# A hybrid SSD and Conformer layer on one core: the second half's loads of split input weights, issued by ScalarE in place of SyncE

## The chip, the cores and the metric

The kernel runs on one core of a Trainium2 chip. The core has five engines, each with its own instruction stream that it works through in order: TensorE (PE: matmuls, with its weight loads as PEld), VectorE (DVE), ScalarE (ACT), GpSimd (POOL) and SyncE (SP), which here does nothing but issue transfers. Transfers (DMAs) run on 16 DMA engines beside them. An engine that issues a transfer first waits, in its own order, until the buffer that the transfer writes is free; the data lands later, and whoever reads it waits for a semaphore. A transfer issued by SP goes into one hardware queue (q1 on the profile's page), one issued by ACT into another (q10).

The metric is device time in microseconds (us) of one execution, and of several runs the median. A profile is of one execution of its own, which has its own time.

## What is computed

One layer over two sequences: 256 context tokens and 2048 latent tokens of width 1024 (18 tiles of 128 tokens). Cut to what matters:

```python
def trunk_layer(x, mod, ...):
    shift, scale, gate = jnp.split(mod, 3, axis=-1)
    h = rms_norm(x, g_pre) * (1 + scale) + shift
    u = h @ w_in
    z, xbc, dt_raw, ga, gb, gsil = jnp.split(u, [...], axis=-1)
    y_ssd, h_fin = ssd_branch(z, xbc, dt_raw, ...)     # conv of 5, scan in both directions, norm
    y_conf = conformer_branch(ga, gb, ...)             # ga * sigmoid(gb), conv of 31, layer norm, silu
    y_conf = y_conf * jax.nn.silu(gsil)
    out = jnp.concatenate([y_ssd, y_conf], axis=-1) @ w_out
    return x + gate * rms_norm(out, g_post), h_fin
```

The product `h @ w_in` is the part that the change touches: the weights that it reads.

## The kernel before

**Split operands.** The input product runs in a fast format, with each operand split into a high part and a low part: h into hh and hl, a weight tile into wh and wl. Each of eight steps over the width of 1024 takes three matmuls (lines 395 to 397): wh by hh, wh by hl, wl by hh.

**Weight tiles.** `w_in` is cut into 44 tiles of 128 columns (`WCOL`): 12 of xbc, 8 of ga, 8 of gb, 8 of z, 8 of gsil. A tile in its two parts takes 512 KB each.

**Two halves.** The tokens are worked in two halves (1280 and 1152 of them), since hh and hl of all do not fit. In the first half, `load_w` reads a tile from `in_w_in`, ScalarE rounds it to wh, VectorE subtracts for wl, and SyncE stores both to the buffers WHD and WLD in memory. In the second half, `load_w` only reads wh and wl back (lines 363 and 364): 44 pairs, 88 transfers.

**Buffers and lookahead.** wh and wl have three buffers each. `next_w` keeps the tile in use and the next two in them: when a unit of work starts, the pair of the tile two further on is asked for, into the buffers that the unit before has used. That load has to wait until PE's last matmul with the old tile is done.

**Units in the second half**, in the order of the program, each of two blocks of 512 tokens (b = 3 and 4), with 24 matmuls per tile and block:
- `xbc_unit` (xp): 12 tiles; ACT copies the sum to `raw` (line 480), then a convolution of 5 runs on ACT and DVE.
- `gab_unit`, 8 of them: tile gb and tile ga. For each block gb's matmuls, ACT's tanh (line 556, `gth`), ga's matmuls, DVE's product, and a store to GL (line 560). So the tiles of one unit are used in turn: gb, ga, gb, ga.
- `silu_unit` (sp), 16 of them: z and gsil, with ACT's tanh at line 571 (`sth`) and a store at line 573.

**What runs beside them.** Interleaved with the gab and z units are the scan over the half's nine latent tiles (`pass_a`) and the grid convolution. In `pass_a`, `load_lb` (line 680) has ACT issue a broadcast load of decay rows into `lb`; GpSimd masks it (692); ACT takes exponents of rows of it (689, tile `el`) and of all of it (700); DVE sums and multiplies (704, 705); PE multiplies with it (736, `py`); DVE closes the sum (777, tile `yg`). The scan's other loads, xT (667) and bc (669), its stores (766, 780) and all transfers of the convolution (kd at 632, cx at 633, the stores cv at 661) are issued by SP. ACT also copies the convolution's kernel rows, `kt` (641).

**What sets the order.** Outside the last stage a scheduler places instructions on each engine by a simulated time, so the order of an engine's stream is not the order of the code. An instruction moved to another engine can shift its new neighbours. Once built, each stream is fixed.

Of the kernel before, what the change touches and what calls it, by code (L numbers as in the profile page):

```python
# [84 lines left out]
def backbone_kernel(ctx, tc, xa, xt_in, cols, rows, wconv, conf_b, gp_row, bg_row, state0, w_mod, w_dt, w_in, w_out,  # L85
                    y_ctx, y_lat, new_state):
    nc = tc.nc
    G, DMA = nc.gpsimd, nc.sync
    V, S, T = (InOrder(tc, e) for e in (nc.vector, nc.scalar, nc.tensor))
# [8 lines left out]
    def dram(name, shape):  # L98
        return drp.tile(shape, F32, tag=name, name=name)
# [12 lines left out]
    WHD = [dram(f"whd{t}", [P, D]) for t in range(len(WCOL))]  # L112
    WLD = [dram(f"wld{t}", [P, D]) for t in range(len(WCOL))]
# [243 lines left out]
    def load_w(half, c0):  # L357
        t = WCOL.index(c0)
        wl = wp.tile([P, KT, P], F32R, tag="wl", name=f"wl{c0}_{half}", bufs=3)
        wh = wp.tile([P, KT, P], F32R, tag="wh", name=f"wh{c0}_{half}", bufs=3)  # L360
        flat = lambda w: w.bitcast(F32).rearrange("p k n -> p (k n)")
        if half:
            DMA.dma_start(flat(wh), WHD[t])
            DMA.dma_start(flat(wl), WLD[t])
            return wh, wl
        for u in range(2):
            ks = slice(4 * u, 4 * u + 4)
            wr = wp.tile([P, 4, P], F32, tag="wr", name=f"wr{c0}_{u}", bufs=2)
            DMA.dma_start(wr.rearrange("p k n -> p (k n)"), w_in[t * P:(t + 1) * P, u * 512:(u + 1) * 512])
            S.copy(wh[:, ks, :], wr)  # L370
            V.tensor_tensor(wl[:, ks, :], wr, wh[:, ks, :].bitcast(F32), SUB)
        DMA.dma_start(WHD[t], flat(wh))
        DMA.dma_start(WLD[t], flat(wl))
        return wh, wl
# [10 lines left out]
    def next_w():  # L385
        while len(wq) < 3 and wcols:
            wq.append(load_w(*wcols.pop(0)))
        return wq.pop(0)
# [726 lines left out]
    def conf_sum(i, n):  # L1115
        v = p2.tile([P, 8, P], F32, tag="v", name=f"v{i}", bufs=2)
        return v, sum8(v[:, 0, :], v[:, 0:4, :], n)
# [174 lines left out]
    v2, t = conf_sum(nx2, n2)  # L1292
# [23 lines left out]
    for a, i in enumerate(order[1:], 1):  # L1316
# [14 lines left out]
        if nx2 is not None:  # L1331
            st_load(nx2)
            v2, t = conf_sum(nx2, n2)
# [113 lines left out]
```

## Time and profile before

| what | value |
|---|---|
| runs of before | 1861.82, 1862.09 and 1856.99 us; median 1861.82 |
| profiled execution | 1866.34 us; span from the first to the last instruction 1864.3 us |
| PE busy over the span | 1809.9 us (97%) |
| DVE, ACT, POOL busy | 1211.3 (65%), 865.3 (46%), 168.4 us (9%) |
| mean granted PE clock | 0.986 |
| queue q1 (SP) | 335.56 MB, 57.8% of 16 engines' span |
| queue q10 (ACT) | 37.76 MB, 7.4% |
| second half's weight loads on SP | first issued at 738.6, last at 1376.5 us |

How to read it: a busy share is an average over stages with different limits, so what a change in one stage is worth is read from that stage. PE's busy time counts pipelined matmuls; the granted clock beside it says how fast they ran. A row of a wait names who waited, for whom, the total, the number of times and the longest. In a timeline a "q" behind an engine's name marks its sequencer, which issues a transfer; the time beside it is that of the issue and not that of the transfer.

### The profile page before, as it was taken

What the parts mean: (1) busy time and instruction counts of PE and PEld (TensorE: products, weight loads), DVE (VectorE), ACT (ScalarE), POOL (GpSimd) and SP (SyncE); (2) the same over time, 40 slices, a digit from 0 to 9 for tenths busy, and PEclk for the clock granted to TensorE, in tenths of its full rate; (3) what the DMA queues carried; (4) which work ended last, traced back from release to release, by engine and by line L of the source; (5) the groups of instructions that cost most, each with busy time, mean ns of one, the idle gap of its engine ahead of it and who ended that gap; (6) DMA issues with size and microseconds to landing.
All of it is one profiled execution on the core that took longest, in us unless ns stands there. A gap on an engine that the chain in (4) does not pass through costs nothing.

```text
span 1864.3 us, 29991 instructions
## 1 busy us (share of the span) xinstructions
PE 1809.9 (97%) x11223; PEld 1492.7 (80%) x11223; DVE 1211.3 (65%) x1841; ACT 865.3 (46%) x1956; POOL 168.4 (9%) x281
## 2 busy tenths in 40 slices
PE   7899999999999999999999989999999999999998
PEld 5788887888888888888887767777887888888886
DVE  2477867565767663587547475869347887777763
ACT  3646424443465441744235344554245545454441
POOL 0002001111111100100001011110000111111110
PEclk8999999999999999999999999999999999999999
DMA  8656565574686664546598879885877666566632
GB/s 299 220 202 207 206 230 187 171 241 151 212 282 227 222 210 160 164 156 201 171 225 234 184 219 230 236 234 196 276 233 247 180 185 171 171 171 171 186 102 79
DMA packets 305309, 375.21 MB, mean 201 GB/s; under 512 B 85255, under 2 KB 204679, under 8 KB 305165
## 3 DMA queue, kind: packets, MB, share of 16 engines
q1 hardware_dynamic: 284428, 335.56, 57.8%
q10 hardware_dynamic: 20736, 37.76, 7.4%
q8 instruction: 88, 1.44, 0.3%
q14 instruction: 57, 0.46, 0.1%
HBM read 243.66 MB, written 129.59 MB: 200 GB/s over the span
## 4 chain that ended last, share of the span: by engine, by line
PE 75%; DMA 12%; DVE 4%; issue 4%; ACT 3%; POOL 1%; SPq 1%; ACTq 0%; POOLq 0%; DVEq 0%
PE op L81 20%; PE sp L395 6%; DMA lb<-lt 6%; PE sp L396 6%; PE sp L397 6%; PE xp L395 4%; PE xp L396 4%; PE xp L397 4%; PE gb L395 2%; PE gb L397 2%; PE gb L396 2%; PE ga L395 2%; PE ga L396 2%; PE ga L397 2%; PE py L736 1%
## 5 line engine op out<-in xcount | busy, mean ns | idle before, releaser
L700 ACT ACTIVATE lb<-lb,WB 128x128 f32<-128x128 f32 x576 | 184.4, 391 | 169.7 <-POOL lb L692 162.5
L395 PE MATMUL sp<-hh,wh 128*128 128x512 f32 (+1 forms) x640 | 239.5, 374 | 0.0
L396 PE MATMUL sp<-hl,wh 128*128 128x512 f32 (+1 forms) x640 | 236.8, 370 | 0.0
L397 PE MATMUL sp<-hh,wl 128*128 128x512 f32 (+1 forms) x640 | 236.6, 370 | 0.0
L395 PE MATMUL xp<-hh,wh 128*128 128x512 f32 (+1 forms) x480 | 178.4, 373 | 6.0 <-ACT wh L370 3.1
L396 PE MATMUL xp<-hl,wh 128*128 128x512 f32 (+1 forms) x480 | 178.2, 372 | 0.0
L397 PE MATMUL xp<-hh,wl 128*128 128x512 f32 (+1 forms) x480 | 178.1, 371 | 0.0
L692 POOL TENSOR_SCALAR_AFFINE_SELECT lb<-lb 128x512 f32<-128x512 f32 x144 | 105.7, 737 | 736.2 <-ACT el L689 412.0
L492 DVE SCALAR_TENSOR_TENSOR cva<-raw,cwh,cva 128x1280 f32<-128x1280 f32 (+1 forms) x96 | 141.6, 1483 | 19.7 <-ACT cva L486 17.7
L395 PEld LDWEIGHTS sp<-hh,wh 128*128 128x128 f32 x640 | 121.4, 190 | 20.6
L397 PEld LDWEIGHTS sp<-hh,wl 128*128 128x128 f32 x640 | 121.2, 189 | 20.9
L396 PEld LDWEIGHTS sp<-hl,wh 128*128 128x128 f32 x640 | 121.3, 190 | 19.9
L395 PE MATMUL ga<-hh,wh 128*128 128x512 f32 (+1 forms) x320 | 121.3, 379 | 6.1 <-DMA wh<-whd 6.1
L75 DVE SCALAR_TENSOR_TENSOR cg<-cg,cv 128x256 f32<-128x256 f32 x240 | 121.2, 505 | 3.4
L395 PE MATMUL gb<-hh,wh 128*128 128x512 f32 (+1 forms) x320 | 121.0, 378 | 2.4 <-DVE gth L559 2.4
L397 PE MATMUL ga<-hh,wl 128*128 128x512 f32 (+1 forms) x320 | 119.6, 374 | 0.1
L397 PE MATMUL gb<-hh,wl 128*128 128x512 f32 (+1 forms) x320 | 119.6, 374 | 0.0
L396 PE MATMUL gb<-hl,wh 128*128 128x512 f32 (+1 forms) x320 | 119.5, 373 | 0.0
L396 PE MATMUL ga<-hl,wh 128*128 128x512 f32 (+1 forms) x320 | 119.2, 372 | 0.0
L704 DVE TENSOR_TENSOR lb<-lb,lb 128x512 f32<-128x512 f32 x72 | 51.2, 711 | 92.9 <-ACT lb L700 77.1
L395 PEld LDWEIGHTS xp<-hh,wh 128*128 128x128 f32 x480 | 91.5, 191 | 23.5 <-ACT wh L370 3.9
L396 PEld LDWEIGHTS xp<-hl,wh 128*128 128x128 f32 x480 | 91.0, 190 | 15.3 <-DVE hl L316 0.4
(254 smaller groups left out, 3744.7 us busy)
## 6 DMA issues: line engine op xcount, KB each, us to landing
lb<-lt ACTq DMA_DIRECT2D x144, 256.0 KB, 4.4
wr<-in_w_in SPq DMA_DIRECT2D x88, 256.0 KB, 5.2
whd<-wh SPq DMA_DIRECT2D x44, 512.0 KB, 3.3
wld<-wl SPq DMA_DIRECT2D x44, 512.0 KB, 5.1
wh<-whd SPq DMA_DIRECT2D x44, 512.0 KB, 5.4
wl<-wld SPq DMA_DIRECT2D x44, 512.0 KB, 5.9
xT<-xb SPq DMA_DIRECT2D x18, 512.0 KB, 4.1
yp<-yg SPq DMA_DIRECT2D x36, 256.0 KB, 6.0
```

What stands on the lines that cost most here:

```text
L75: return self._tc.keep_in_program_order(getattr(self._eng, name)(*a, **k))
L81: return lambda *a, **k: self._tc.keep_in_program_order(f(*a, **k))
L395: T.matmul(ps[:, :BN], wh[:, k, :], hh[:, k, :], start=(k == 0), stop=False)
L396: T.matmul(ps[:, :BN], wh[:, k, :], hl[:, k, :], start=False, stop=False)
L397: T.matmul(ps[:, :BN], wl[:, k, :], hh[:, k, :], start=False, stop=(k == KT - 1))
L492: V.scalar_tensor_tensor(a[:, :n], raw[:, t:t + n], cwh[:, ct * 5 + t:ct * 5 + t + 1], a[:, :n], MUL, ADD)
L692: G.affine_select(E[g, hq, d], E[g, hq, d], pattern=[[0, 4], [sg, P]], compare_op=ALU.is_ge, fill=NEG, base=0, channel_multiplier=-sg)
L700: S.activation(lb[:, h, :], lb[:, h, :], AF.Exp, bias=WB[:, i, c + h:c + h + 1])
L704: V.tensor_tensor(a, a, E[g, hq, 1], ADD)
L736: T.matmul(py[g][j * HD:(j + 1) * HD, q * P:(q + 1) * P], xt[g][:, h * HD:(h + 1) * HD], E[g, hq, 0][:, t, :], start=True, stop=True)
```

## The change

Two lines of `load_w`: in the second half the pair is issued by ACT (`S`) and no longer by SP (`DMA`).

```diff
         if half:
-            DMA.dma_start(flat(wh), WHD[t])
-            DMA.dma_start(flat(wl), WLD[t])
+            S.dma_start(flat(wh), WHD[t])
+            S.dma_start(flat(wl), WLD[t])
             return wh, wl
```

All sizes, buffers and the first half stay. PE's stream keeps its order but for three groups of small matmuls of the step sizes that stand two or four matmuls later. Names in the rows below end in numbers of the buffer or tile: whd_137 and wld_181 are the parts of the fifth further ga tile (GA5; GA0 is whd_132), whd_146 is GB6, whd_136 GA4, whd_145 GB5.

ACT's stream where the pair of GA5 stands now, ahead of the tanh of the fifth gab unit's second block (gth_4_4); rows with + are new there:

```order
 L700 ACTIVATE lb_10434<-lb_10434,WB 128x128 x4
 L680 DMA lb_10109<-lt_116 128x512
+L363 DMA wh_1_9664<-whd_137 128x1024
+L364 DMA wl_1_9663<-wld_181 128x1024
 L556 ACTIVATE gth_4_4_10015<-gb_4_4_9890 128x512
 L689 ACTIVATE el_9876<-lb_10109 64x256 x2
 L680 DMA lb_10179<-lt_116 128x512
```

The pair stands between an lb load and the tanh that waits for the same block of matmuls as the pair does; the next lb load is four rows behind it.

SP's stream at the same place in the program, from which the pair of GA5 and the one of GB6 are taken; a row with - is gone from where it stood:

```order
 L632 DMA kd_10813<-in_wconv 32x1024 x3
 L669 DMA bc_10330<-xb_64 128x4x128
-L363 DMA wh_1_9664<-whd_137 128x1024
-L364 DMA wl_1_9663<-wld_181 128x1024
+L766 DMA st_108<-sb_10074 128x512
 L780 DMA yp_90<-yg_9703 128x512
-L766 DMA st_108<-sb_10074 128x512
-L363 DMA wh_1_10125<-whd_146 128x1024
-L364 DMA wl_1_10124<-wld_190 128x1024
 L667 DMA xT_10328<-xb_64 128x8x128
 L560 DMA gl_72<-gth_4_4_10015 128x512
```

GA5's pair stood behind the convolution's kd loads and the scan's bc load; without the pairs the scan's two stores change places, and xT and gl follow at once.

ACT's stream one unit earlier, where the pair of GA4 stands now, in the new order alone:

```order
L700 ACTIVATE lb_10111<-lb_10111,WB 128x128 x4
L363 DMA wh_1_9195<-whd_136 128x1024
L364 DMA wl_1_9194<-wld_180 128x1024
L556 ACTIVATE gth_3_4_9530<-gb_3_4_9353 128x512
L716 COPY xt_9630<-px_9513 128x512
L680 DMA lb_10181<-lt_116 128x512
```

The pair stands directly ahead of its unit's tanh (gth_3_4), and an lb load comes two rows behind that tanh.

## The prediction

> **What bounds the kernel now.** I read the page first, then the busy time by stage, then what TensorE (PE) waits for inside the second half, and last the timelines around the one wait that the change can touch. The stages are mine: 735 to 920 us are the second half's first twelve weight tiles, 920 to 1290 the weight tiles that run beside the state-space scan and the grid convolution, 1290 to 1415 the rest of the second half. Columns: length, busy us of each engine, granted clock, DMA share, GB/s.
>
> ```profile
> span 1864.3 us, 29991 instructions
> ...
> core 0: us, PE busy (x) PEld busy (x) DVE busy (x) ACT busy (x) POOL busy (x), PEclk, DMA share, GB/s
> 735.00:920.00 185.00, 185.00 (x866) 154.94 (x865) 122.90 (x136) 90.58 (x156) 10.96 (x25) 1.00 0.50 167
> 920.00:1180.00 260.00, 241.66 (x2410) 190.50 (x2408) 152.76 (x263) 113.13 (x275) 28.41 (x47) 0.96 0.88 219
> 1180.00:1290.00 110.00, 105.20 (x1016) 83.33 (x1015) 87.78 (x151) 60.68 (x152) 16.60 (x21) 0.97 0.78 233
> 1290.00:1415.00 125.00, 123.40 (x839) 101.42 (x838) 62.23 (x92) 38.93 (x75) 1.10 (x2) 1.00 0.73 233
> ```
>
> PE is the bound. It is busy in all of the first stage at full clock, and in all but 1.6 us of the last. Only from 920 to 1290 does it stand: 18.3 + 4.8 = 23.1 us, and the clock is granted at 0.96 and 0.97. The change can gain only there. What ended PE's waits in the second half (total us, times, longest):
>
> ```profile
> PE px L712 <- issue: 6.4, 3, 2.9
> PE ga L395 <- DMA wh<-whd: 6.1, 1, 6.1
> PE po L743 <- DVE yg L777: 3.2, 1, 3.2
> PE cp L652 <- DVE yg L777: 2.8, 1, 2.8
> PE pst L749 <- ACT sb L765: 1.3, 1, 1.3
> ...
> PE cp L652 <- ACT sb L765: 0.9, 1, 0.9
> ...
> PE pst L749 <- ACT xwh L726: 0.4, 1, 0.4
> ```
>
> Of 44 pairs of weight loads just one is ever waited for: 6.1 us. It is the pair of the fifth gated tile (GA5, whd_137). First the queue that issued it (SP), then PE:
>
> ```profile
> 1055.27 0.32 SPq L560 DMA_DIRECT2D gl<-gth  x1
> 1064.65 0.34 SPq L632 DMA_DIRECT2D kd<-in_wconv  x1
> 1065.09 4.36 SPq L661 DMA_DIRECT2D cv<-cvv  x4
> 1069.49 3.26 SPq L632 DMA_DIRECT2D kd<-in_wconv  x3
> 1072.85 0.39 SPq L669 DMA_DIRECT2D bc<-xb  x1
> 1073.34 0.45 SPq L363 DMA_DIRECT2D wh<-whd  x1
> 1073.88 0.38 SPq L364 DMA_DIRECT2D wl<-wld  x1
> ...
> SPq L632 <- ACT kt L641: 9.0, 1, 9.0
> ```
>
> ```profile
> 1059.89 0.40 PE L397 MATMUL gb<-hh,wl 128*128 128x512 f32 x1
> ...
> 1072.43 0.39 PE L395 MATMUL gb<-hh,wh 128*128 128x512 f32 x1
> ...
> 1074.93 0.39 PE L397 MATMUL gb<-hh,wl 128*128 128x512 f32 x1
> 1081.41 0.77 PE L395 MATMUL ga<-hh,wh 128*128 128x512 f32 x1 [6.09 <-DMA wh<-whd]
> ...
> 1085.81 0.48 PE L395 MATMUL ga<-hh,wh 128*128 128x512 f32 x1
> ```
>
> The buffer of GA5 was free when PE left it at 1060.3 (the gb matmul of 1059.89, 0.40 long). SP issued the load at 1073.34, 13 us later, because it stood in order behind a kd load (9.0 us of waiting for ScalarE's kt copy), four cv stores and more kd loads. PE wanted it at 1075.3 and had it at 1081.4. Behind the wait PE ran slow: the 12 matmuls from 1081.41 to 1085.81 took 4.40 us, where 11 steps from 1072.43 to 1074.93 took 2.50, 0.227 each, so 2.73 for 12. That is 1.7 us more, and the stall costs 6.1 + 1.7 = **7.8 us**.
>
> **What the change removes.** SP loses 88 issues; ScalarE (ACT) gains them. In ACT's new order GA5's pair stands behind the lb load of 1066.12 and directly ahead of the gth of 1067.24:
>
> ```profile
> 1066.12 0.38 ACTq L680 DMA_DIRECT2D lb<-lt  x1
> ...
> 1067.24 0.58 ACT L556 ACTIVATE gth<-gb 128x512 f32<-128x512 f32 x1
> ...
> 1073.24 0.36 ACTq L680 DMA_DIRECT2D lb<-lt  x1
> ...
> 1081.12 0.84 ACT L689 ACTIVATE el<-lb 64x256 f32<-64x256 f32 x2 [4.60 <-DMA lb<-lt]
> ```
>
> So it goes out at about 1066.5 to 1066.9. The landing times of L363, then of L364, then of the lb loads with the time that ACT's queue takes for one issue:
>
> ```profile
> DMA to landing us min/median/max: 3.7/5.4/7.9
> ...
> DMA to landing us min/median/max: 4.5/5.9/7.9
> ...
> L680 ACTq DMA_DIRECT2D lb<-lt x144: 326/326/1619, 149.1 to 1279.9; - x144
> ...
> DMA to landing us min/median/max: 3.0/4.4/9.1
> ```
>
> With the worst, 7.9, wh lands at 1074.4 and wl at 1074.8, still ahead of 1075.3. Term one: **-7.8 us**, and nothing else of this pair is late in its place.
>
> Every other pair keeps its cover in the old order, but loses some in the new one, for ACT runs behind PE here. The thinnest is GA4, which goes ahead of the gth of 1027.94 and is wanted at 1033.61:
>
> ```profile
> 1027.94 0.57 ACT L556 ACTIVATE gth<-gb 128x512 f32<-128x512 f32 x1
> ...
> 1033.61 0.39 PE L395 MATMUL ga<-hh,wh 128*128 128x512 f32 x1
> ```
>
> Issued near 1027.3, it lands between 1031.0 and 1035.2: a wait of 0 to 1.6 us. At the median of 5.4 (1032.7) it is none, and I take 0.
>
> **What it adds.** Three costs, each bounded from both sides.
>
> The issues. No row shows a weight load on ACT; the nearest is the lb row, 0.326 us each (1.619 at most), so 88 x 0.326 = 28.7 us of ACT's time, at worst 142. ACT is busy 303.3 of the 680 us in the four stages, so nearly all lies beside PE's work; with that cover gone the 28.7 us would be on the path. PE waited for ACT three times that count (1.3, 0.9 and 0.4 us in the rows above). A pair ahead of each makes them 3 x 0.65 = 2.0 us longer. I take half, **+1.0**; the ends are 0 and 28.7.
>
> The waits. A load waits until PE has left the buffer, and everything behind it on ACT (tanh, masks' exponents, state copies, lb loads) waits too. Ahead of a gth or sth this is free: that instruction waits for the same block of matmuls. Elsewhere ACT comes later than PE: GA5's buffer was free at 1060.3 and ACT gets there at 1066.5. I take 0. The upper end is SP's own longest wait of this kind between 920 and 1290, 9.4 us once.
>
> ```profile
> SPq L363 <- PE ga L397: 9.4, 1, 9.4
> ...
> L363 SPq DMA_DIRECT2D wh<-whd x22: 319/420/1609, 924.1 to 1285.2; - x22
> ...
> ACT lb L700 <- POOL lb L692: 66.8, 36, 7.0
> ACT el L689 <- DMA lb<-lt: 31.3, 11, 6.1
> ```
>
> The queue. The rows above are of the stretch 920 to 1290. The lb loads feed the scan: they land, GpSimd masks, ACT takes exponents, VectorE mixes, PE multiplies. ACT's two waits on that chain make 66.8 + 31.3 = 98.1 us of the 370. A pair is now 1 MB in the same queue ahead of an lb load, where it was in SP's queue beside it. If the queue is served in order, an lb load issued right behind a pair lands after the pair's 5.9 us and its own 256 KB. Half a megabyte against a quarter is 5.9 - 4.4 = 1.5, so 7.4 and not 4.4: 3.0 us later. In ACT's new order 14 of the 22 pairs that SP issued in this stretch have an lb load one or two rows behind them: 14 x 3.0 = 42 us of lateness in the chain. What share reaches PE? Its waits for VectorE's yg, the end of the chain, are 3.2 + 2.8 = 6.0 us against ACT's 98.1, or 0.061. So I take 42 x 0.061 = **+2.6**. The upper end is all 42. The lower end is below nothing: at 1073.24 ACT waited 4.60 us for an lb load while SP issued two weight loads, which now leave at other times, so -4.6.
>
> The Trainium skill, *DMA: Bandwidth & Descriptors*, section "Queues, rings and completion order", says that SP and ACT each own one row of rings on the same 16 DMA engines and that each engine consumes a ring in order; by it the 3.0 us would hold for every lb load that closely follows a pair. No run here shows such a case yet.
>
> Sum: -7.8 + 1.0 + 2.6 = **-4.2 us**. The profiled execution took 1866.34 us, 2.1 more than its span, and would come to 1862.1. It lies 4.5 us above the median of the three runs (1861.82), so some of what I counted may be missing in a typical run. I take the same 4.2 off the median: **1857.6 us**.
>
> **The rivals.**
>
> *Only the issuer changes.* All loads but one were covered, and if the GA5 stall belongs to this execution alone, or moves to GA4 (1.6 us), what is left is the given-back 1.0 + 2.6 less what SP's freedom may bring: between -1 and +4 us, 1861 to 1866. For it: the profiled execution is slower than the median. Against it: the 13 us on SP come from program order, not from a chance of landing. The skill's page *DMA: Bandwidth & Descriptors*, section "Issuing engines are not separate DMA queues", sides with it: issuing from several engines saves the sequencer's time alone. By that rule the gain would be 0; the SP rows above bear it out on the transfer and not on the wait, which was the queue's.
>
> *The scan is starved (the slower side).* Place: the same 22 pairs, in the queue that the lb loads share. If 0.4 of the 42 us reaches PE, that is 16.8, and with the issues 17.8; less 7.8 makes +10: 1872, and 1867 to 1880 around it. It is slower than before from a share of (7.8 - 1.0) / 42 = 0.16, and slower by over 0.3% from 0.30. For it: from 920 to 1180 the DMA engines are busy at 0.88, and ACT waits 98.1 us on that chain already. Against it: the share was 0.061 so far.
>
> *SP's freedom does more.* Without 88 issues and their waits, stores and the loads of bc, xT and cx leave earlier, and the lb loads lose a competitor. If half of the other 17.0 us of PE's standing time goes (8.5), and its slow matmuls in the same proportion as at GA5 (1.7 / 6.1, so 2.4), the gain is 7.8 + 10.9 less 1.0: -17.7, 1844, and 1839 to 1852 around it. For it: SP waits 9.0 us behind one copy. Against it: px, the largest wait, names no DMA.
>
> **How the numbers follow.** A measurement of this kernel tells about 0.3% from no change, 5.6 us. The forecast (-8 to 0 us) has 0.42, of which 0.15 lies beyond 0.3%. Only the issuer: 0.14. Starved: 0.24, of which 0.02 within 0.3%. Freedom: 0.20. So faster 0.15 + 0.20 = 0.35, same 0.27 + 0.14 + 0.02 = 0.43, slower 0.22. The range runs from 1843 to 1874: the forecast and the issuer case whole, and somewhat more than half of each of the other two, whose middles are 1844 and 1872. It leaves out some 0.18. The forecast's own range is 1853 to 1862.
>
> **What would show it.** Right: PE's wait for wh is gone or under 2 us, the weight loads stand in ACT's queue at 0.33 us each, PE's standing time from 920 to 1290 falls from 23 to some 20 us, and the stages 735 to 920 and 1290 to 1415 keep their length. The queue term shows in the landing median of the lb loads, above 4.4, and in ACT's wait for lb, above 31. Wrong: a new PE wait for wh at another tile, a wait of ACT for PE behind a weight load, or more PE waits for yg and sb.

## The result, and the profile after

The change makes the kernel **slower**: 1872.25 us, the median of six runs (1867.96 to 1876.52), against 1859.70 for six runs of before on the same chip (1855.54 to 1862.09). The ratio is 1.0070, its 95% interval 1.0055 to 1.0085, so some 13 us. The profiled execution took 1873.18 us, only 6.8 more than the one of before (1866.34), which lay 4.5 us above the median of its kernel's runs, as the prediction had noted.

The stages of after, in the columns of the prediction (length, busy us of each engine, granted clock, DMA share, GB/s):

```profile
core 0: us, PE busy (x) PEld busy (x) DVE busy (x) ACT busy (x) POOL busy (x), PEclk, DMA share, GB/s
735.00:920.00 185.00, 183.46 (x858) 153.32 (x857) 121.32 (x134) 90.65 (x156) 11.86 (x25) 1.00 0.50 166
920.00:1180.00 260.00, 245.24 (x2448) 194.53 (x2448) 160.16 (x274) 114.47 (x280) 29.55 (x48) 0.97 0.90 226
1180.00:1290.00 110.00, 101.11 (x988) 80.23 (x989) 82.67 (x142) 59.40 (x149) 15.93 (x20) 0.95 0.75 219
1290.00:1415.00 125.00, 120.19 (x809) 98.32 (x808) 57.04 (x82) 37.67 (x73) 0.55 (x1) 0.97 0.73 225
```

Both kernels are cut at the same times here, not at the same instructions. PE stands less in 920 to 1180 (14.8 us, before 18.3), but more in the two stages behind it: 8.9 us where it was 4.8, and 4.8 where it was 1.6; from 735 to 920, where it was always busy, it stands 1.5. In the two behind 1180 the granted clock is lower as well, 0.95 (0.97) and 0.97 (1.00). So something was gained among the ga and gb units, and more was lost among the z units (1180 to 1290) and the gsil units (1290 to 1415). What ended PE's waits in the second half of after (total us, times, longest):

```profile
PE pst L749 <- DVE cvv L656: 4.9, 1, 4.9
PE px L712 <- issue: 4.9, 2, 3.9
PE si L177 <- ACT woh L986: 4.6, 1, 4.6
PE px L712 <- DVE cvv L656: 3.5, 2, 2.9
PE pst L749 <- ACT sb L765: 3.0, 1, 3.0
...
PE ga L397 <- DMA wl<-wld: 2.1, 1, 2.1
PE xp L397 <- DMA wl<-wld: 1.5, 1, 1.5
```

The wait for wh is gone; 2.1 us of wl of the same tile are left, and 1.5 us for wl of an xbc tile (xp) are new. Two waits have grown at the head. One is for `cvv`, a sum of the grid convolution on DVE: 4.9 and 3.5 us, before 0.6 and 0.6. The other is that of `si` (the scan's start state, turned by PE) for `woh`, a rounded tile of output weights: 4.6 us, before 0.7.

**The loss at 1358, in the gsil units.** SP's and ACT's queues around the third gsil pair. First before, from SP's timeline (start, length of the issue, engine, line), then after, from SP's and from ACT's:

```profile
1319.29 0.62 SPq L766 DMA_DIRECT2D st<-sb  x1
1319.96 0.43 SPq L363 DMA_DIRECT2D wh<-whd  x1
1320.43 0.50 SPq L364 DMA_DIRECT2D wl<-wld  x1
...
1323.51 0.32 SPq L1020 DMA_DIRECT2D stl<-st  x1
```

```profile
1319.11 0.65 SPq L766 DMA_DIRECT2D st<-sb  x1
1319.81 0.70 SPq L780 DMA_DIRECT2D yp<-yg  x1
1328.91 0.32 SPq L1020 DMA_DIRECT2D stl<-st  x1
```

```profile
1318.02 0.35 ACTq L363 DMA_DIRECT2D wh<-whd  x1
...
1318.45 0.51 ACTq L364 DMA_DIRECT2D wl<-wld  x1
```

SP's own waits, among them the row for the load of stl behind the store of sb, before and after:

```profile
SPq L980 <- DMA yp<-yg: 4.2, 1, 4.2
...
SPq L1020 <- DMA st<-sb: 1.9, 1, 1.9
```

```profile
SPq L1020 <- DMA st<-sb: 8.3, 1, 8.3
```

The last stage reads back a state that the scan has just stored (`stl<-st`), so SP waits until the store has landed. Before, the pair left 0.7 us behind that store. After, it left 1.1 us ahead of it. 1 MB of weights that nobody wants for two units now precedes 256 KB that SP, and with it everything in SP's order, waits for.

That wait alone moves the loads of the output weights (`wst`, line 980) only a little, though they stand behind stl in SP's order. Counted from the issue of the store of sb, stl leaves after 9.8 us in place of 4.2, but the first wst after 10.8 in place of 9.3, because before, SP stood 4.2 us there for a store of yg (the first row above). More is lost further on. The fifth to seventh wst, before and then after, with two loads of `z` (line 1016) ahead of them:

```profile
1335.80 0.68 SPq L1016 DMA_DIRECT2D z<-zs  x1
1336.58 3.35 SPq L363 DMA_DIRECT2D wh<-whd  x1
1340.02 0.38 SPq L364 DMA_DIRECT2D wl<-wld  x1
1340.49 0.86 SPq L980 DMA_DIRECT2D wst<-in_w_out  x2
...
1341.91 0.38 SPq L980 DMA_DIRECT2D wst<-in_w_out  x1
```

```profile
1333.66 7.44 SPq L1016 DMA_DIRECT2D z<-zs  x2
1341.19 4.72 SPq L980 DMA_DIRECT2D wst<-in_w_out  x2
...
1346.49 0.37 SPq L980 DMA_DIRECT2D wst<-in_w_out  x1
```

So the seventh wst leaves 27.4 us after the store in place of 22.6. ACT's `woh` follows it, and PE's si starts after 38.9 us in place of 34.4. SP's own order differs there as well: in all seven profiled kernels that move the pair of the store, both loads of y stand ahead of both loads of z, which take turns in the eleven others. How much of the delay comes from the store, from the later pairs and from this order was not separated.

**The loss in the z units.** ACT's timeline of after at two places:

```profile
1211.45 0.33 ACTq L363 DMA_DIRECT2D wh<-whd  x1
...
1211.90 1.19 ACTq L364 DMA_DIRECT2D wl<-wld  x1
...
1213.47 0.33 ACTq L680 DMA_DIRECT2D lb<-lt  x1
...
1220.04 0.84 ACT L689 ACTIVATE el<-lb 64x256 f32<-64x256 f32 x2 [5.50 <-DMA lb<-lt]
```

```profile
1254.73 0.34 ACTq L363 DMA_DIRECT2D wh<-whd  x1
...
1255.20 0.36 ACTq L364 DMA_DIRECT2D wl<-wld  x1
...
1255.60 0.44 ACTq L680 DMA_DIRECT2D lb<-lt  x1
...
1263.45 0.84 ACT L689 ACTIVATE el<-lb 64x256 f32<-64x256 f32 x2 [5.96 <-DMA lb<-lt]
```

Here a load of lb directly follows a pair in ACT's own queue, and ACT starts on it 6.6 and 7.9 us after its issue, having stood 5.5 and 6.0 us for it. The median landing of all lb loads from 920 to 1290 did not move (4.7 us before, 4.6 after), so this is a matter of two places and not of the stretch.

How this reaches PE is not shown. From 1195 to 1295 PE stands 2.9 us for cvv (before, not at all), and 3.9 us with no cause named (before, 4.7 in two waits); no row names lb. Waits of this length for lb also occur without a pair ahead in the queue: 6.1 us at most from 920 to 1290 before, and 5.9 us at 1274 in the kernel below that moves five gsil pairs alone. What the two pairs cost is told by the runs with just these two.

### The profile page after: what moved, and what is told of

The parts are those of the page before. It is cut to its first block, busy times and chain, and to the rows that moved or that the text cites. A ratio compares the mean times of both kernels' runs of the same rounds, so it can differ in the third digit from the quotient of the medians.

```text
span 1871.4 us, 29958 instructions
## 1 busy us (share of the span) xinstructions
PE 1809.4 (97%) x11223; PEld 1493.9 (80%) x11223; DVE 1210.7 (65%) x1841; ACT 866.1 (46%) x1956; POOL 171.5 (9%) x281
## 3 DMA queue, kind: packets, MB, share of 16 engines
q10 hardware_dynamic: 33408, 83.90, 14.8%
## 4 chain that ended last, share of the span: by engine, by line
PE 78%; DMA 11%; DVE 3%; issue 3%; ACT 3%; POOL 1%; SPq 0%; ACTq 0%; POOLq 0%; DVEq 0%
PE op L81 20%; PE sp L395 6%; PE sp L396 6%; PE sp L397 6%; PE xp L395 4%; PE xp L397 4%; PE xp L396 4%; DMA lb<-lt 4%; PE gb L395 3%; PE gb L397 3%; PE gb L396 3%; PE ga L395 2%; PE ga L397 2%; PE ga L396 2%; PE py L736 2%
## 5 line engine op out<-in xcount | busy, mean ns | idle before, releaser
L397 PEld LDWEIGHTS xp<-hh,wl 128*128 128x128 f32 x480 | 91.1, 190 | 17.1 <-DMA wl<-wld 2.0
```

Source lines behind the costliest of these rows:

```text
L397: T.matmul(ps[:, :BN], wl[:, k, :], hh[:, k, :], start=False, stop=(k == KT - 1))
```

## The experiments

Pairs are numbered in the order of WCOL: xbc 0 to 11, ga and gb 12 to 27, z 28 to 35, gsil 36 to 43. Every experiment is the kernel before with some pairs issued by another engine, in lines 363 and 364 alike, so the diffs show line 363 only; S is ACT, DMA is SP and G is GpSimd. All ratios are to runs of before on the same chip, with 95% intervals; microseconds are the ratio less 1, times the median of before. The ratio is not the quotient of the two medians, and the difference of the medians can lie up to 2.5 us away from the value in the table.

| pairs on ACT | runs | ratio | us |
|---|---|---|---|
| 0-11 (xbc) | 4 | 1.0000 [0.9982, 1.0018] | 0.0 |
| 12-27 (ga, gb) | 4 | 0.9984 [0.9968, 0.9999] | -3.0 |
| 28-35 (z) | 4 | 1.0039 [1.0023, 1.0055] | +7.3 |
| 36-43 (gsil) | 4 | 1.0050 [1.0030, 1.0070] | +9.3 |
| 32, 34 | 12 | 1.0015 [1.0003, 1.0028] | +2.8 |
| 38 | 12 | 1.0017 [1.0005, 1.0029] | +3.2 |
| all but 32, 34, 38 | 12 | 1.0020 [1.0002, 1.0039] | +3.7 |
| 32, 34, 38 on GpSimd | 12 | 1.0014 [1.0000, 1.0028] | +2.6 |
| 38, 39, 40 | 12 | 1.0025 [1.0011, 1.0039] | +4.7 |
| 36, 37, 41-43 | 12 | 1.0002 [0.9988, 1.0015] | +0.4 |
| 28-31, 33, 35 | 12 | 1.0003 [0.9990, 1.0016] | +0.6 |
| 0-27 | 12 | 0.9975 [0.9962, 0.9989] | -4.7 |
| all 44 | 7 | 1.0060 [1.0038, 1.0081] | +11.2 |
| 0-35 | 12 | 1.0012 [0.9994, 1.0031] | +2.2 |
| 0-27, 36-43 | 12 | 1.0031 [1.0013, 1.0048] | +5.8 |
| all but 32, 34, 38, 39, 40 | 12 | 1.0001 [0.9985, 1.0018] | +0.2 |

**One group of units at a time.** Theory 1: lb loads stand behind pairs in the shared queue. Theory 2: pairs leave earlier and crowd SP's urgent transfers. Theory 3: the 88 issues on ACT cost, in proportion to their number.

```diff
-DMA.dma_start(flat(wh), WHD[t])
+(S if t < 12 else DMA).dma_start(flat(wh), WHD[t])
```

> Only the 12 pairs of the xbc tiles are issued by ScalarE, the other 32 by SyncE as before; TensorE's stream is that of the change but for its later part. Theory 1, the shared queue (an lb load stands behind a pair in ScalarE's queue): only four lb loads lie near these pairs, so 0 to +2 us. Theory 2, crowding (a pair now leaves at once in a queue of its own and takes half of the DMA engines from urgent transfers of SyncE): here the urgent ones are the ht loads at the start of the half; the profile of the change had lost 2 us more there than before, so +2 to +3 us. Theory 3, ScalarE's order (issues and waits in its stream, in proportion to the pairs): 12/44 of 12.6, +3.4 us.

```diff
-DMA.dma_start(flat(wh), WHD[t])
+(S if 12 <= t < 28 else DMA).dma_start(flat(wh), WHD[t])
```

> Only the 16 pairs of the ga and gb tiles are issued by ScalarE; TensorE's stream is that of before. In the two profiles the change gained 8 to 9 us in this stretch. Theory 1: the lb loads behind these pairs cost what the change lost, so +6 us or more. Theory 2: kd, cx and cv of SyncE are crowded, 0 to +4 us. Theory 3: 16/44 of 12.6, +4.6 us. If the gain of the two profiles is real in most executions, -6 to -8 us; if the wait for wh was peculiar to the profiled execution of before, about 0.

```diff
-DMA.dma_start(flat(wh), WHD[t])
+(S if 28 <= t < 36 else DMA).dma_start(flat(wh), WHD[t])
```

> Only the 8 pairs of the z tiles are issued by ScalarE; TensorE's stream is that of before. The profile of the change lost 6 us between 1214 and 1310, with two waits of ScalarE of 5.5 and 6.0 us for an lb load issued 0.4 to 1.6 us behind a pair. Theory 1: +4 to +7 us. Theory 2: 0 to +2 us. Theory 3: 8/44 of 12.6, +2.3 us.

```diff
-DMA.dma_start(flat(wh), WHD[t])
+(S if t >= 36 else DMA).dma_start(flat(wh), WHD[t])
```

> Only the 8 pairs of the gsil tiles are issued by ScalarE; TensorE's stream is that of before. No lb load is left in this stretch. The profile of the change lost 7 us between 1330 and 1372, with a TensorE wait of 4.6 us behind the splitting of the output weights, whose loads SyncE issues. Theory 1: 0. Theory 2: +5 to +7 us. Theory 3: +2.3 us.

Measured: 0, -3.0, +7.3 and +9.3 us. Theory 3 falls: 28 pairs cost nothing or gain, and eight cost 9 us. The four add up to +13.6, the whole change to +13.0 on its own chip. What is left is to tell whether every pair of the last sixteen costs something, or a few cost all.

**The pairs that overtake.** Theory A: only a pair that now leaves ahead of an urgent transfer costs, and costs a whole stall. Theory B: each costs its share.

```diff
-DMA.dma_start(flat(wh), WHD[t])
+(S if t in (32, 34) else DMA).dma_start(flat(wh), WHD[t])
```

> Only two of the 44 pairs are issued by ScalarE: the fifth and the seventh of the z units (pairs 32 and 34); everything else is as before. In the trace with all eight z pairs on ScalarE these two left directly ahead of a load of lb in the same queue (wl at 1219.4, lb at 1220.7; wl at 1261.2, lb at 1262.1), and those loads landed 7.3 and 8.0 us after their issue, with ScalarE waiting 6.15 and 6.49 us for them; no other z pair had a load of lb within 3 us behind it. Theory A (an urgent transfer that a pair overtakes costs a whole stall, other pairs cost nothing): nearly the whole loss of the eight, +7 us (+4 to +9) against before. Theory B (every pair costs its share): 2/8 of it, +1.8 us. Theory C (the z units lose through something else, such as SyncE running ahead): no rule for these two, 0 to +2 us.

```diff
-DMA.dma_start(flat(wh), WHD[t])
+(S if t in (38,) else DMA).dma_start(flat(wh), WHD[t])
```

> Only one of the 44 pairs is issued by ScalarE: the third of the gsil units (pair 38). With all eight gsil pairs on ScalarE it left at 1314.0, 1.2 us ahead of the store of sb that SyncE issued at 1315.2, and SyncE's next load (stl) waited 7.1 us for that store; before, the pair left 0.7 us behind the store and the wait was 1.9 us. Theory A (this one overtaking is the loss): about the whole loss of the eight, +9 us (+4 to +10); the wait of SyncE for st<-sb about 7 us and PE's wait for woh about 4.5 us. Theory B (every pair its share): 1/8, +1.1 us, and SyncE's wait for the store near 2 us.

```diff
-DMA.dma_start(flat(wh), WHD[t])
+(DMA if t in (32, 34, 38) else S).dma_start(flat(wh), WHD[t])
```

> All pairs on ScalarE but the three named (32, 34 and 38), which SyncE issues as before: 41 of 44 moved. Theory A: the loss is gone and what is left is the sum of the xbc and the ga/gb pairs alone, -3 us (-6 to 0) against before. Theory B: 41/44 of +13, that is +12 us. If freeing SyncE is what hurts (theory C): +10 us or more.

```diff
-DMA.dma_start(flat(wh), WHD[t])
+(G if t in (32, 34, 38) else DMA).dma_start(flat(wh), WHD[t])
```

> Only the three pairs 32, 34 and 38 are moved, and to GpSimd, so that they pass through neither SyncE's nor ScalarE's queue. Theory A1 (order inside one queue: lb stands behind the pair that left ahead of it on ScalarE): the two losses in z are gone, since lb no longer shares a queue with the pairs; pair 38 still leaves ahead of the store of sb in a queue of its own, so its loss stays: about +9 us (+4 to +10). Theory A2 (the transfers crowd each other on the shared DMA engines whatever their queue): both losses, +16 us (+10 to +18), as far as GpSimd issues them as early as ScalarE did. If GpSimd reaches them later than ScalarE did, neither loss: 0 us.

Measured: +2.8, +3.2, +3.7 and +2.6 us. The first two lie between the theories, and below the ranges that A gave (+4 at least). The third is a miss for A, which said -3, and for B and C, which said +10 or more. (The expectation of the first says that no other z pair has an lb load within 3 us behind it. Pair 35 has one 1.1 us behind it in the same profile, issued at 1276.50; ACT's wait there ended with a DVE result and not with lb.) The profiles say more. Two waits mark the loss in the gsil units: that of SP for the store of sb (its waits from 1295 to 1375) and that of PE's si for woh (PE's waits from 735 to 1430), in us, here with three kernels of the later series. The last three columns are times from the issue of the store of sb to that of the first wst, to that of the seventh, and to PE's si:

| pairs on ACT | SP for st<-sb | PE si for woh | first wst | seventh wst | si |
|---|---|---|---|---|---|
| none (before) | 1.9 | 0.7 | 9.3 | 22.6 | 34.4 |
| all (the change) | 8.3 | 4.6 | 10.8 | 27.4 | 38.9 |
| 38 | 7.9 | 2.8 | 10.3 | 26.3 | 36.9 |
| 32, 34, 38 on GpSimd | 7.0 | none | 9.2 | 24.8 | 36.1 |
| all but 32, 34, 38 | 2.1 | 2.8 | 9.2 | 24.8 | 36.7 |
| 38, 39, 40 | 7.2 | 4.2 | 9.6 | 26.7 | 38.1 |
| 36, 37, 41-43 | 2.2 | none | 8.9 | 22.2 | 34.0 |
| all but 32, 34, 38, 39, 40 | 2.4 | none | 8.1 | 22.1 | 33.8 |

Pair 38 does what A says to SP: alone on ACT it makes SP wait 7.9 us, and back on SP it doesn't. In all 18 profiles of this case SP waits 6.5 to 8.3 us for that store where 38 is moved (seven kernels), and 1.9 to 2.4 us where it is not (eleven). But with 38 on SP and 41 others on ACT, PE waits for woh all the same, so another pair delays the output weights too. The candidates are 39 and 40, which before stood behind or among the wst loads in SP's order: 40 now leaves ahead of two that it stood behind. That profile, of an execution of 1874.17 us, the slowest of its twelve, also shows a third kind of victim. SP's timeline, with the store of yg:

```profile
1232.99 0.54 SPq L780 DMA_DIRECT2D yp<-yg  x1
```

ACT's, with pair 33:

```profile
1232.35 0.33 ACTq L363 DMA_DIRECT2D wh<-whd  x1
...
1234.48 0.34 ACTq L364 DMA_DIRECT2D wl<-wld  x1
```

DVE's, where the profile puts its wait down to the store of yg:

```profile
1244.39 0.69 DVE L772 TENSOR_TENSOR yg<-xT,dcol 128x512 f32<-128x512 f32 x1 [6.26 <-DMA yp<-yg]
```

Pair 33 left around that store. DVE went on 11.4 us after the store's issue, and PE waited 4.7 us for yg. In before that store left at 1233.06, the pair behind it at 1235.47, and DVE went on at 1239.08, 6.0 us after the store's issue. In the profile of the whole change the store (1228.41) left 1.1 us ahead of pair 33, and DVE didn't wait for it: which of the two leaves first is not the same in every kernel.

Issued by GpSimd, pair 38 left 1.0 us ahead of the store as well, in neither SP's nor ACT's queue, and SP waited 7.0 us. PE's si came late as well (36.1 us; the profile names the load of si's own input, 2.6 us, and not woh). So it is neither ACT's work nor a shared queue that makes the store late: what the kernels have in common is that 1 MB leaves 1 us ahead of it. Whether lb is spared when its pair goes by GpSimd the time can't tell (+2.6, 0.0 to +5.2, under both of A's numbers). In the profiles ACT stood 3.1 us for the first of the two lb loads, and 5.9 us with 32 and 34 on ACT, one execution each.

**Closing the two stages.**

```diff
-DMA.dma_start(flat(wh), WHD[t])
+(S if t in (38, 39, 40) else DMA).dma_start(flat(wh), WHD[t])
```

> Three of the 44 pairs are issued by ScalarE: pairs 38, 39 and 40 of the gsil units. 38 goes ahead of the store of sb that the load of stl waits for; 39 and 40 go ahead of loads of the output weights (wst) that they stood behind or among in SyncE's queue. Theory A (only pairs that overtake an urgent transfer cost): the whole loss of the eight gsil pairs, +8 us (+6 to +10), since pair 38 alone gave +4 and, in the trace with 38 back on SyncE, some +3.7 us were still lost between 1340 and 1372. Theory B (every pair its share): 3/8 of +9, +3.4 us, no more than pair 38 alone gave.

```diff
-DMA.dma_start(flat(wh), WHD[t])
+(S if t in (36, 37, 41, 42, 43) else DMA).dma_start(flat(wh), WHD[t])
```

> The other five gsil pairs (36, 37, 41, 42 and 43) on ScalarE, 38 to 40 on SyncE as before. Theory A: nothing, 0 us (-2 to +2); the landmarks between 1295 and 1372 keep their distance to those of before. Theory B: 5/8 of +9, +5.6 us. Theory C (SyncE, freed of the pairs, issues its other transfers earlier and these get in the way): about 5/8 too.

```diff
-DMA.dma_start(flat(wh), WHD[t])
+(S if t in (28, 29, 30, 31, 33, 35) else DMA).dma_start(flat(wh), WHD[t])
```

> The other six z pairs (28 to 31, 33 and 35) on ScalarE, 32 and 34 on SyncE as before. The eight together cost +7 us, 32 and 34 alone +3.8. Theory A: pair 33 left, in the trace with 41 pairs moved, 0.6 us ahead of the store of yg, which then took 11 us to land in place of 6, so this one may cost a stall; the other five nothing: +3 us (0 to +5), with the loss between 1231 and 1254 if there is one. Theory B: 6/8 of +7, +5.3 us, spread over the stretch from 1150 to 1290.

```diff
-DMA.dma_start(flat(wh), WHD[t])
+(S if t < 28 else DMA).dma_start(flat(wh), WHD[t])
```

> The 28 pairs of the xbc, ga and gb units on ScalarE, the 16 of z and gsil on SyncE as before. If the parts add up (0 for xbc, -3 us for ga and gb): -3 us (-5 to 0) against before, faster than both kernels. If every pair costs (theory B): 28/44 of +12, +8 us. PE's wait for wh in the ga units, 6.1 us before, should be gone or under 1 us, and the wait for wl there about 2 us.

Measured: +4.7, +0.4, +0.6 and -4.7 us. The five gsil pairs cost nothing, as A has it and B (+5.6) does not; SP waits as before, and PE has no wait for woh. The other three gave +4.7 [2.0, 7.3], about half of what the eight gave. That is a miss for A, whose range was +6 to +10, and the interval also holds B's +3.4; only the five tell the two apart. Their profile has both waits, SP's and then PE's:

```profile
SPq L1020 <- DMA st<-sb: 7.2, 1, 7.2
```

```profile
PE si L177 <- ACT woh L986: 4.2, 1, 4.2
```

The six z pairs cost nothing measurable either (B: +5.3), pair 33 among them, though in their profile it again left ahead of the store of yg (1228.38 and 1228.98) and PE waited 3.1 us for yg. That execution (1865.93 us) is 3.3 us above the median of its kernel, so its profile may not show the usual course. The 28 pairs alone are **faster than both kernels**: 1858.88 us against 1861.95, ratio 0.9975 [0.9962, 0.9989]. PE's waits for ga weights in their profile:

```profile
PE ga L397 <- DMA wl<-wld: 2.0, 1, 2.0
...
PE ga L395 <- DMA wh<-whd: 0.2, 1, 0.2
```

In all ten profiles of kernels that leave the ga and gb pairs on SP, that of before among them, PE waits 4.3 to 6.2 us for wh there, so the stall is a fixture of the old order. These pairs have a price too: PE's wait for cvv at line 749 is 1.8 to 5.4 us in the eight profiles with them on ACT, 4.2 or more in six of these, and 0.6 to 2.6 in the ten. What makes cvv late is open.

**Do the parts add up?** The small sets on their own came to about +4 us in all, the change to +13.

```diff
-DMA.dma_start(flat(wh), WHD[t])
+S.dma_start(flat(wh), WHD[t])
```

> The whole change once more, all 44 pairs on ScalarE, in more rounds and beside the next three on one chip. If the parts add up as measured one by one: +4 us (+1 to +8) against before. If there is a loss that only the parts together have: +9 us or more (its six runs gave +12.6).

```diff
-DMA.dma_start(flat(wh), WHD[t])
+(S if t < 36 else DMA).dma_start(flat(wh), WHD[t])
```

> The 28 pairs of xbc, ga and gb and the eight of z on ScalarE, gsil on SyncE. Adding up: -4.7 + 2.8 + 0.6 = -1.3 us (-4 to +3; +2.5 if the eight z pairs together cost the 7 us of their four runs). If the z stretch suffers more when the units ahead of it are moved too: +5 us or more.

```diff
-DMA.dma_start(flat(wh), WHD[t])
+(DMA if 28 <= t < 36 else S).dma_start(flat(wh), WHD[t])
```

> The 28 pairs of xbc, ga and gb and the eight of gsil on ScalarE, z on SyncE. Adding up: -4.7 + 4.7 + 0.4 = +0.4 us (-3 to +4). If gsil suffers more in company: +5 us or more.

```diff
-DMA.dma_start(flat(wh), WHD[t])
+(DMA if t in (32, 34, 38, 39, 40) else S).dma_start(flat(wh), WHD[t])
```

> 39 of the 44 pairs on ScalarE; 32, 34, 38, 39 and 40, the five that were found to overtake an urgent transfer, on SyncE as before. If these five carry the loss and the rest adds up: -4.7 + 0.6 + 0.4 = -3.7 us (-6 to 0), faster than both kernels. If every pair costs, or the parts together have a loss of their own: +4 us or more, near the whole change.

Measured: +11.2, +2.2, +5.8 and +0.2 us. The first and the third lie on the side of a loss that the small sets lack (+9 and +5 or more), the second within the range of mere adding up, the fourth just above it. By stages the change adds up: the 28 pairs -4.7; z on top of them +6.9 (2.2 against -4.7), alone +7.3; gsil on top +10.5, alone +9.3; so -4.7 + 7.3 + 9.3 = +11.9, and the whole is +11.2. Within a stage it does so only loosely: two and six z pairs give 2.8 + 0.6 where eight give 7.3, three and five gsil pairs 4.7 + 0.4 where eight give 9.3, with intervals of some 2.5 to 4 us to either side. By differences of medians, for which there are no intervals, the sets fit better (4.2 + 0.7 and 5.6; 5.4 + 1.2 and 6.8; all five sets +8.5, the whole +9.2), so noise may be all that is missing. But the last two kernels are beside each other on one chip: putting five of the 44 pairs back on SP takes the change from +11.2 to +0.2, so **these five carry the 11 us** in the company of the others. Alone they came to 2.8 + 4.7 = 7.5. Why 39 moved pairs then stand at +0.2 [-2.8, +3.3] and not at the -3.7 expected is open; the two intervals meet at their ends.

## Why the prediction failed

The forecast was 1857.6 us, -4.2, and the change is +13. The time lies in the range, at the middle of the rival in which the scan is starved, but that is luck. Less than half of the loss arose in the z units, where this mechanism can act (+7.3 of 7.3 + 9.3), and its way to PE is not shown there; in the gsil units no lb load is left.

- **GA5, -7.8: right mechanism, size off.** The wait for wh is gone. But ACT did not issue the pair at 1066.5 to 1066.9; from after's timeline of ACT:

```profile
1070.64 0.33 ACTq L363 DMA_DIRECT2D wh<-whd  x1
1071.55 0.42 ACTq L364 DMA_DIRECT2D wl<-wld  x1
1072.02 0.60 ACT L556 ACTIVATE gth<-gb 128x512 f32<-128x512 f32 x1 [4.57 <-DMA cv<-cvv]
```

  and of PE, at the wait:

```profile
1079.10 0.50 PE L397 MATMUL ga<-hh,wl 128*128 128x512 f32 x1 [2.10 <-DMA wl<-wld]
```

  ACT had finished the exponents ahead of the pair at 1067.5 and stood 3 us before it issued. The profile puts the whole pause down to SP's stores of cvv (line 661), the first of which left at 1064.70. In all eight profiles with this pair on ACT it left 5.5 to 6.2 us behind that store, and in seven the profile names it, so the pair seems to have waited for it; this was not tested. wl landed at 1079.1, and PE ran slow behind that wait as well: the steps from 1080.18 to 1083.17 took 0.43 us each and not 0.23, 1.4 us more for seven. So 2.1 + 1.4 = 3.5 of the 7.8 stayed and 4.3 were gained at this wait. PE's wait of 4.9 us for cvv lies just ahead of it (at 1062.46; before 0.6), and over the stage PE stands only 3.5 us less; the 28 pairs together gained 4.7 [2.0, 7.1].
- **The issues, +1.0, and the waits of ACT, 0: small, as said.** The eleven z and gsil pairs that were moved without the five cost 0.6 + 0.4 us, within the noise, and the twelve of xbc 0.0. The issues are 0.326 us each, as taken from the lb row. The 3 us of standing at GA5 belong to the second of these terms and were set at nothing.
- **The queue, +2.6: the mechanism was there, its places and weight were not.** The term spread 3.0 us over 14 pairs and let 0.061 of the sum through. The landing median that was to show it (over 4.4) says nothing: it was 4.7 in this stretch before and is 4.6 after (over the whole kernel, 4.4 and 4.6); ACT's wait for lb did rise, from 31.3 to 40.8 us. What counted were two z pairs with an lb load directly behind, +2.8 [0.6, 5.2] by themselves, and the z units together +7. By these times far more than 0.061 of the lateness reached PE there, if it came by lb. The Trainium skill, *DMA: Bandwidth & Descriptors*, "Queues, rings and completion order", says that a DMA engine consumes the descriptors of one ring in their order, so those of an lb load come behind those of a pair ahead of it in ACT's ring. The two lb rows above, 6.6 and 7.9 us from issue to use, agree with it.
- **The step that failed: the transfers of SP that the pairs overtake had no term.** The prediction asked what stands behind the pairs in the queue they enter, and whether GA5's own data comes in time. It did not ask which transfers of the queue they leave stood *ahead* of them and would now stand behind on the same DMA engines. "The change can gain only there" (920 to 1290) was taken to mean that it can lose only there, and 1290 to 1415 was to keep its length. There pair 38 went ahead of the store that SP waits for (8.3 us in place of 1.9), and 39 and 40 left beside the output weights, whose seventh load came 4.8 us later: +9.3 us for the eight gsil pairs, the larger part of the loss. The row of PE that shows it is si for woh, 4.6 us in place of 0.7. Behind that wait PE ran slow: si and the nine steps after it took 5.5 us in place of 3.0. Together this makes some 6 of the 9 us.
- The rival "SP's freedom does more" had it the wrong way round: SP, freed of the pairs, stood 8.3 us for one store.

Whether more buffers for sb and yg would take the stores off the path was not tried.

## What to carry over

When a bulk transfer is moved to another queue, list not only what it will delay in the new queue but what it stood behind in the old one: that order was a priority. Early loads with two units of slack should be left behind the stores and loads that somebody waits for, and moved only where they stand behind something blocked (here the ga and gb units, -4.7 us). A stage in which the bound engine never stands has nothing to gain from such a move and all its slack to lose.

## What the runs showed of the hardware

- A store of 256 KB that takes 4.2 us from issue to where SP goes on (1319.29 to 1323.51), with 1 MB leaving 0.7 us behind it, takes 9.8 (1319.11 to 1328.91) when the 1 MB leaves on another queue 1.1 us ahead of it. With the 1 MB on GpSimd's queue, 1.0 us ahead, it takes 8.2. Separate queues did not keep the two apart.
- PE ran slow for a while behind three of its waits, at 0.43 us a step in place of 0.23. That cost 1.7 us behind the 6.1 us for wh before, 1.4 us behind the 2.1 us for wl after, and 2.5 us behind the 4.6 us for woh after.
